# A decoder block's expert-table stage: instructions written out in turn, and four smaller edits

## The chip, the cores and the metric

The kernel runs on one core of a Trainium2 chip. The metric is device time in microseconds of one launch. One launch of the kernel before was also profiled; its trace is what the prediction reads. Five engines work side by side, each through its own instructions in order: TensorE (PE; PEld is its weight load), VectorE (DVE), ScalarE (ACT), GpSimd (POOL) and SyncE (SP, which here only issues DMAs). They wait for one another through semaphores.

## The reference

One decoder block on 1024 tokens of 1024 channels. Two mixers run side by side (an RWKV-7 recurrence and an attention over selected keys), are merged and normalised; then comes the part that matters here, a mixture of 16384 one-neuron experts:

```python
q = (ht @ w_pq).reshape(T, 8, 2, 64)                  # 8 heads, two half queries
s = jnp.einsum('thcd,hcnd->thcn', q, sub_keys)        # 128 first and 128 second keys
s1, i1 = lax.top_k(s[:, :, 0], 16); s2, i2 = lax.top_k(s[:, :, 1], 16)
cand = (s1[..., :, None] + s2[..., None, :]).reshape(T, 8, 256)
top_s, pos = lax.top_k(cand, 16)                      # 16 of 256 pairs
experts = take_along_axis(i1*128 + i2, pos)           # expert = first key * 128 + second key
gates = softmax(top_s)
act = gelu(einsum('cd,chkd->chk', h, u_tab[experts])) * gates
out = einsum('chk,chkd->cd', act, v_tab[experts])
```

A second residual and layer norm follow. Everything is float32.

## The kernel before

A scheduler puts the instructions of each engine in order when the program is built: it takes the order in which the code is written as priority and moves an instruction ahead where its own clock says that the earlier ones would still wait. On the chip each engine then keeps that order. Tiles come from pools with a fixed number of buffers (`bufs`); a new tile waits until the oldest buffer of that name is free.

The experts are computed in two ways. The first 384 tokens (three tiles of 128, `NG = 3`) are **gathered**: for each of 128 slots a row of 128 expert vectors is fetched with an indirect DMA on GpSimd (L1371, 512 KB each) into a room `g` and used by one VectorE instruction (L1375 for the dot with the token, L1379 for the weighted sum). These are 768 rows. Rows 0 to 127 are tied to earlier work, and row 300 (`MIDDLE`) is the first that may use a room of the last stage. Three rooms `g` serve them until then. The other 640 tokens (five tiles, 3 to 7) are **dense**: every expert is computed for every token and multiplied by a gate that is zero for experts not chosen. TensorE multiplies in float32 pieces: each operand is split into a high and a low part, ScalarE copying the high part (`whi`, L233) and GpSimd subtracting for the low part (`wlo`, L1272), and three products are added (L1285, L1287, L1289). One unit of dots, for 128 experts that share a first key, is 48 matmuls.

The stages around the change, in order of time:

- **Merge of the second half** (`merge`, H = 1). Eight output-projection units (L1044 on VectorE writes `vt`), a layer norm with transposes (L1063, L1108, L1114, L1070), then eight units of the expert queries (`wq`). Between units `next(side)` advances the retrieval of tiles 1 and 2, one of twelve steps after each of the first twelve units.
- **Retrieval** (`retrieve`): top 16 of each key half with MAX8, MATCH_REPLACE8 and FIND_INDEX8 on VectorE (L1136 to L1173), then the rank arithmetic: for each of six sums per tile `weighted` multiplies (L1190) and halves the 16 columns in four adds (L1192, L1194, L1195, L1196).
- **Table stage.** For each of the five dense tiles `gate_table` runs 16 steps of 8 tokens. A step makes two sets of one-hot rows: second keys in one instruction for eight tokens (L1247), first keys times gate for each token, six by VectorE (L1252) and two by two ScalarE instructions each (L1254, L1255). Eight float32 matmuls (L1259, two records each in the trace) give tables, which ScalarE copies from PSUM, transposing in its write (`st<-tp`, L233), and a DMA stores (`gtD`). The retrieval of tiles 3 to 7 feeds it; transposes (L1236) hand the found keys over. The same stage computes 69 units of dots ahead of their use (`dots_u`, stored by `dotD<-ds`) and gather rows 128 to 299. In the code the dots come after all tables and the gather at the very end of the program; the scheduler fills them in.
- **Dense stage.** For each of 16 groups of eight first keys: `dense_u` (dots, or `al`, the stored ones, then gelu, times the gate table `gt`, L1315, then split into `A`, the low part by L1317) and `dense_v` of the group before (eight units of 48 matmuls). Gate tables are loaded for four first keys at a time into two buffers (L1644, 1.3 MB each). In each group but the first the code puts one unit that is not stored ahead (`lead`) in front.

## Time and profile before

| | us |
|---|---|
| median of 3 runs | 3887.53 (3887.27 to 4839.4) |
| the profiled execution | 3874.22 |
| its span, first to last instruction | 3872.5 |
| PE / DVE / ACT / POOL busy | 3549.4 / 2759.5 / 1611.5 / 1992.2 |

Busy time is the union of an engine's instructions. Shares are averages over stages that differ much: the profile's slices show PE at nine tenths almost everywhere, and DVE at nine tenths or more only in the table stage. Times in the rows below count from the start of the span.

### The profile page before, as it was taken

The page shows a single profiled execution, that of the slowest core. Times are in us where ns is not written, and L with a number is a line of the kernel's source. Part 1 is how long each engine was busy: PE and PEld are TensorE (multiplying, and loading weights), DVE is VectorE, ACT ScalarE, POOL GpSimd, SP SyncE. Part 2 cuts the span into 40 slices and gives each one's busy share as a digit, 9 for nine tenths or more (in the row PEclk, how much of TensorE's full clock was granted, in tenths as well). Part 3 has the DMA queues.
Part 4 walks back from the last instruction along what each step waited for, and adds up shares of the span by engine and source line. Part 5 has one row for each costly group of instructions (what it writes and reads, how often), then busy time and mean ns, then how long its engine had stood idle before and what let it go on. Part 6 is the DMA issues. An engine that isn't in the chain of part 4 may idle for free.

```text
span 3872.5 us, 65040 instructions
## 1 busy us (share of the span) xinstructions
PE 3549.4 (92%) x24044; PEld 3172.0 (82%) x24045; DVE 2759.5 (71%) x5983; ACT 1611.5 (42%) x2909; POOL 1992.2 (51%) x1566
## 2 busy tenths in 40 slices
PE   8989999888999998779999898899999999999997
PEld 7667776665777776669889898899999999999997
DVE  7856644857377767779999999566676666676654
ACT  3558852343444443426455463622222232222222
POOL 5442222355455543254545454266676676776655
PEclk9999998999999999889999999999999999999998
DMA  7453334765676765477777777688898988998973
GB/s 231 148 151 103 103 98 143 280 188 183 192 222 219 218 220 170 140 258 261 243 259 252 258 273 248 234 301 314 310 332 317 330 313 323 335 323 318 322 266 115
DMA packets 434994, 920.97 MB, mean 238 GB/s; under 512 B 36356, under 2 KB 195412, under 8 KB 431732
## 3 DMA queue, kind: packets, MB, share of 16 engines
q1 hardware_dynamic: 311956, 498.38, 38.5%
q0 software_dynamic: 122720, 418.43, 31.0%
q8 instruction: 190, 3.11, 0.3%
q14 instruction: 128, 1.05, 0.1%
HBM read 791.59 MB, written 125.08 MB: 237 GB/s over the span
## 4 chain that ended last, share of the span: by engine, by line
PE 33%; DVE 21%; DMA 19%; issue 10%; POOL 9%; ACT 4%; SPq 1%; POOLq 0%; ACTq 0%; DVEq 0%
DMA g<-in_v_dram,gidx 4%; PE acc L425 4%; PE acc L426 4%; PE acc L427 4%; DMA g<-in_u_dram,gidx 4%; POOL g L1371 4%; POOL wlo L1272 4%; DVE pg L1379 3%; DMA raw<-in_vt_dram 3%; DMA gt<-gtD 3%; DVE gt L1252 3%; PE pair L1285 2%; PE pair L1287 2%; PE pair L1289 2%; DMA raw<-in_ut_dram 2%
## 5 line engine op out<-in xcount | busy, mean ns | idle before, releaser
L1272 POOL TENSOR_TENSOR wlo<-raw,whi 128x1024 fp32r<-128x1024 f32 x264 | 641.0, 2429 | 285.8 <-ACT whi L233 273.6
L415 POOL TENSOR_TENSOR wlo<-wraw,whi 128x512 fp32r<-128x512 f32 x280 | 372.5, 1333 | 564.0 <-ACT whi L233 496.7
L1371 POOL DMA_INDIRECT g<-in_u_dram,gidx x384 | 403.8, 1052 | 374.0 <-DVE g L1375 211.5
L1371 POOL DMA_INDIRECT g<-in_v_dram,gidx x384 | 388.0, 1011 | 378.3 <-DVE pg L1379 192.2
L1379 DVE SCALAR_TENSOR_TENSOR pg<-g,dots,pg 128x1024 f32<-128x1024 f32 x381 | 489.3, 1284 | 120.3 <-DMA g<-in_v_dram,gidx 113.9
L1285 PE MATMUL pair<-A,whi 128*128 128x320 f32 (+2 forms) x2048 | 483.0, 312 | 38.7 <-DVE A L1317 25.9
L1285 PE MATMUL pair<-h2T,whi 128*128 128x320 f32 x2048 | 479.1, 314 | 17.3 <-DMA h2T<-h2TD 10.0
L1287 PE MATMUL pair<-h2T,whi 128*128 128x320 f32 x2048 | 482.1, 315 | 3.7 <-DMA h2T<-h2TD 3.7
L233 ACT ACTIVATE whi<-raw 128x1024 fp32r<-128x1024 f32 x264 | 278.4, 1056 | 496.2 <-PE pair L1287 194.6
L1287 PE MATMUL pair<-A,whi 128*128 128x320 f32 (+2 forms) x2048 | 480.8, 311 | 0.0
L1289 PE MATMUL pair<-A,wlo 128*128 128x320 f32 (+2 forms) x2048 | 480.2, 311 | 0.5 <-POOL wlo L1272 0.5
L1289 PE MATMUL pair<-h2T,wlo 128*128 128x320 f32 x2048 | 480.4, 314 | 0.0
L1375 DVE SCALAR_TENSOR_TENSOR g<-g,pg 128x1024 f32<-128x1024 f32 x256 | 308.3, 1216 | 106.8 <-DMA g<-in_u_dram,gidx 104.6
L1285 PEld LDWEIGHTS pair<-A,whi 128*128 128x128 f32 x2048 | 348.8, 190 | 43.3 <-issue 29.6
L425 PE MATMUL acc<-big,whi 128*128 128x512 f32 x864 | 356.3, 413 | 23.5 <-DVE zs L533 7.1
L1285 PEld LDWEIGHTS pair<-h2T,whi 128*128 128x128 f32 x2048 | 348.3, 191 | 20.2 <-issue 11.0
L1287 PEld LDWEIGHTS pair<-h2T,whi 128*128 128x128 f32 x2048 | 349.5, 191 | 5.5 <-DMA h2T<-h2TD 4.0
L427 PE MATMUL acc<-big,wlo 128*128 128x512 f32 x864 | 350.7, 406 | 2.4 <-POOL wlo L415 2.4
L426 PE MATMUL acc<-big,whi 128*128 128x512 f32 x864 | 348.9, 404 | 3.6 <-DVE big L451 3.6
L1289 PEld LDWEIGHTS pair<-h2T,wlo 128*128 128x128 f32 x2048 | 348.8, 191 | 1.5
L1289 PEld LDWEIGHTS pair<-A,wlo 128*128 128x128 f32 x2048 | 348.8, 190 | 1.0 <-POOL wlo L1272 1.0
L1287 PEld LDWEIGHTS pair<-A,whi 128*128 128x128 f32 x2048 | 349.2, 190 | 0.0
(482 smaller groups left out, 6650.4 us busy)
## 6 DMA issues: line engine op xcount, KB each, us to landing
raw<-in_vt_dram SPq DMA_DIRECT2D x136, 512.0 KB
raw<-in_ut_dram SPq DMA_DIRECT2D x128, 512.0 KB
gtD<-st SPq DMA_DIRECT2D x20, 2048.0 KB
gt<-gtD SPq DMA_DIRECT2D x32, 1280.0 KB
wraw<-in_wz_dram SPq DMA_DIRECT2D x152, 256.0 KB
dotD<-ds SPq DMA_DIRECT2D x69, 320.0 KB
al<-dotD SPq DMA_DIRECT2D x69, 320.0 KB
mw<-in_wada_dram SPq DMA_DIRECT2D x32, 512.0 KB
```

The source lines that it names most:

```text
L233: copy = lambda o, i, **k: A.activation(o, i, AF.Copy, **k)
L415: G.tensor_tensor(lo, raw, hi.bitcast(F32), op=OP.subtract)
L425: mm(pt, lhsT=wh[:, ks], rhs=ah[:, k, :], start=k == 0, stop=False)
L426: mm(pt, lhsT=wh[:, ks], rhs=al[:, k, :], start=False, stop=False)
L427: ins = mm(pt, lhsT=wl[:, ks], rhs=ah[:, k, :], start=False, stop=k == nk - 1)
L1272: G.tensor_tensor(lo, raw, hi.bitcast(F32), op=OP.subtract)
L1285: mm(pts[n], lhsT=wh, rhs=ah[:, h], start=k == 0, stop=False)
L1287: mm(pts[n], lhsT=wh, rhs=al[:, h], start=False, stop=False)
L1289: mm(pts[n], lhsT=wl, rhs=ah[:, h], start=False, stop=last)
L1371: G.indirect_dma_start(out=u, out_offset=None, in_=a["u" if n < 2 else "v"], in_offset=bass.IndirectOffsetOnAxis(ap=idx[:, k:k + 1], axis=0))
L1375: V.scalar_tensor_tensor(u, u, 1.0, h2, op0=OP.mult, op1=OP.mult, accum_out=dots[:, k:k + 1])
L1379: V.scalar_tensor_tensor(acc, u, dots[:, k:k + 1], acc, op0=OP.mult, op1=OP.add)
```

## The change

- The table stage is written out in turn: 30 times one retrieval step, three table steps of each tile at hand, two units of dots and four gather rows; then eight times two table steps, one unit and four or no rows; then what is left. The gather becomes a generator (`gather_all`) that starts in this stage. Rows 128 to 299 use six rooms: three `g` and three `gx`.
- In a table step the first-key one-hots of eight tokens come from one bfloat16 comparison on VectorE (`hot`, against `keys8`, iota repeated eight times), and eight ScalarE copies multiply each by its gate. The two-instruction form on ScalarE, `iotan` and `ng` are gone. The matmuls write their columns to PSUM four apart, and the copy out of PSUM reads them in line and writes runs of four.
- In `weighted` one TENSOR_REDUCE takes the place of the four adds.
- In the second merge the twelve retrieval steps stand after every other unit, four of them in the `wq` loop.
- `h2T`, the dense tokens, is loaded in eight pieces (both parts of one 128-channel slice each) in place of two.
- `lead` is gone: the first keys of a group stand in their order, stored ones first.

```diff
-            if H or d % QS == QS - 1:
+            if H == 0 or d % 2:
                 next(side, None)
...
-            next(side, None)
+            if H == 0 or d % 2:
+                next(side, None)
...
             nc.sync.dma_start(qTD[H][:, h, :], qt)
+            if H and h % 2 == 0:
+                next(side, None)
...
-            V.tensor_tensor(pr[:, :, 0:8], pr[:, :, 0:8], pr[:, :, 8:16], op=OP.add)
-            s4 = tp_.tile([128, 64, 8], F32, name="wx")
-            V.tensor_tensor(s4[:, :, 0:4], pr[:, :, 0:4], pr[:, :, 4:8], op=OP.add)
-            V.tensor_tensor(s4[:, :, 0:2], s4[:, :, 0:2], s4[:, :, 2:4], op=OP.add)
-            V.tensor_tensor(dst, s4[:, :, 0], s4[:, :, 1], op=OP.add)
+            V.tensor_reduce(dst, pr, axis=AX.X, op=OP.add)
...
-            oh = du.tile([128, 16, 128], F32, name="gt", bufs=2)
-            V.tensor_tensor(oh[:, 0:8], iota[:, None, :].to_broadcast([128, 8, 128]),
-                            slots[:, 1, b * 8:b * 8 + 8, None].to_broadcast([128, 8, 128]), op=OP.is_equal)
+            room = du.tile([128, 20, 128], F32, name="gt", bufs=2)
+            oh2, oh1 = room[:, 0:8], room[:, 8:16]
+            hot = room[:, 16:20].rearrange("p a b -> p (a b)").bitcast(BF).rearrange("p (a b) -> p a b", b=8)
+            V.tensor_tensor(hot, keys8, k1[:, None, b * 8:b * 8 + 8].to_broadcast([128, 128, 8]), op=OP.is_equal)
+            V.tensor_tensor(oh2, iota[:, None, :].to_broadcast([128, 8, 128]),
+                            slots[:, 0, b * 8:b * 8 + 8, None].to_broadcast([128, 8, 128]), op=OP.is_equal)
             for t in range(8):
-                c = slice(b * 8 + t, b * 8 + t + 1)
-                if t < ONE_HOT:
-                    V.tensor_scalar(oh[:, 8 + t], iotan, slots[:, 0, c], slots[:, 2, c], op0=OP.is_equal, op1=OP.mult)
-                else:
-                    A.activation(oh[:, 8 + t], iota, AF.Square, bias=slots[:, 0, c])
-                    A.activation(oh[:, 8 + t], oh[:, 8 + t], AF.Relu, scale=ng[:, c], bias=slots[:, 2, c])
+                copy(oh1[:, t], hot[:, :, t], scale=slots[:, 1, b * 8 + t:b * 8 + t + 1])
             for u in range(2):
-                tp = ptp()
+                tp = ptp().rearrange("p (a b) -> p a b", b=4)
                 for t in range(4):
-                    mm(tp[:, t * 128:(t + 1) * 128], lhsT=oh[:, 4 * u + t], rhs=oh[:, 8 + 4 * u + t], start=True, stop=True)
+                    mm(tp[:, :, t], lhsT=oh2[:, 4 * u + t], rhs=oh1[:, 4 * u + t], start=True, stop=True)
                 t0 = b % 4 * 8 + 4 * u
-                copy(s_[:, :, t0:t0 + 4].rearrange("p a b -> p b a"), tp.rearrange("p (b a) -> p b a", b=4))
+                copy(s_[:, :, t0:t0 + 4], tp)
...
+        def room(row):
+            if EARLY <= row < MIDDLE and row % (GB + GX) >= GB:
+                return at["sl"].tile([128, 1024], F32, name="gx", bufs=GX)
...
-        for n in range(2):
-            G.dma_start(h2T[:, n], h2TD[:, n])
+        for k in range(8):
+            G.dma_start(h2T[:, :, k], h2TD[:, :, k])
...
+            def beside(tables, dots, n):
+                for g in list(found.values()):
+                    for _ in range(tables):
+                        next(g, None)
+                for _ in range(dots):
+                    next(ahead_, None)
+                for _ in range(n):
+                    next(rows)
+            steps = 6 * (8 - M1)
+            n = (MIDDLE - EARLY) // (steps + 6)
+            for k in range(steps):
+                next(side)
+                beside(3, 2, n)
...
+            for k in range(8):
+                beside(2, 1, n if k < 6 else 0)
...
-                    lead = next(i1 for i1 in first if i1 not in ahead)
-                    first = [lead] + [i1 for i1 in first if i1 != lead]
```

On VectorE, the start of the tables of tile 3, before (`pg<-g,dots,pg` is a gather row, `gt<-iota` the second keys, `gt<-iotan` the first keys):

```order
L1247 TENSOR_TENSOR gt<-iota,slots 128x1024
L1252 TENSOR_SCALAR gt<-iotan,slots 128x128 x6
L1379 SCALAR_TENSOR_TENSOR pg<-g,dots,pg 128x1024
L1247 TENSOR_TENSOR gt<-iota,slots 128x1024
L1252 TENSOR_SCALAR gt<-iotan,slots 128x128 x6
L1379 SCALAR_TENSOR_TENSOR pg<-g,dots,pg 128x1024 x2
```

The same place now (`gt<-keys_15512` is the bfloat16 comparison, `gx` one of the three new rooms):

```order
L1250 TENSOR_TENSOR gt<-iota,slots 128x1024
L1249 TENSOR_TENSOR gt<-keys_15512,slots 128x1024 x2
L1250 TENSOR_TENSOR gt<-iota,slots 128x1024
L1393 SCALAR_TENSOR_TENSOR pg<-gx,dots,pg 128x1024 x3
L1393 SCALAR_TENSOR_TENSOR pg<-g,dots,pg 128x1024 x3
L1249 TENSOR_TENSOR gt<-keys_15512,slots 128x1024
L1250 TENSOR_TENSOR gt<-iota,slots 128x1024
L1393 SCALAR_TENSOR_TENSOR pg<-gx,dots,pg 128x1024 x2
```

Six instructions per step have become one, and more gather rows stand between steps. Between one tile's hand-over to TensorE and the next, the four table cycles of the stage held 14.9 to 15.7 units of dots each in TensorE's order; now they hold 17.5, 15.8, 15.0 and 12.6, and VectorE's order 57, 51, 42 and 21 gather rows, 171 in place of 150.

On VectorE, the second merge where its layer norm begins (`lnst` is the norm, `vt` the last output projections, all else the retrieval), before:

```order
L1184 TENSOR_TENSOR ge<-wx,ranks 128x1024
L1190 TENSOR_TENSOR wp<-ge,df 128x1024
L1044 SCALAR_TENSOR_TENSOR vt<-acc,modc,xt 128x512
L1108 BN_STATS lnst<-rw 128x6
L1192 TENSOR_TENSOR wp<-wp 128x64x8
L1108 BN_STATS lnst<-rw 128x6 x2
L1194 TENSOR_TENSOR wx<-wp 128x64x4
L1109 BN_AGGR lnst<-lnst 128x2 x2
L1195 TENSOR_TENSOR wx<-wx 128x64x2
L1190 TENSOR_TENSOR wp<-ge,ranks 128x1024
```

And now:

```order
L1193 TENSOR_REDUCE i_14527<-wp 128x64
L1216 SCALAR_TENSOR_TENSOR i_14526<-i_14526,i_14527 128x128
L1218 CAST idx<-i_14526 128x128
L1042 SCALAR_TENSOR_TENSOR vt<-acc,modc,xt 128x512 x2
L1109 BN_STATS lnst<-rw 128x6 x3
L1110 BN_AGGR lnst<-lnst 128x2 x2
L1112 RECIPROCAL lnst<-lnst 128x1 x2
L1113 SCALAR_TENSOR_TENSOR lnst<-lnst 128x1 x2
```

The rank arithmetic of tile 2 no longer stands among the norm's instructions; it now comes behind them.

On SyncE, one group of the dense stage (`gt<-gtD` loads a gate table, `raw` weights, `al` stored dots), before:

```order
L1268 DMA raw<-in_ut_dram 128x1024 x2
L1308 DMA al<-dotD 128x640
L1644 DMA gt<-gtD 128x20x128
L1308 DMA al<-dotD 128x640
L1268 DMA raw<-in_vt_dram 128x1024 x3
L1644 DMA gt<-gtD 128x20x128
L1268 DMA raw<-in_vt_dram 128x1024 x2
```

And now:

```order
L1267 DMA raw<-in_ut_dram 128x1024
L1307 DMA al<-dotD 128x640
L1687 DMA gt<-gtD 128x20x128
L1267 DMA raw<-in_ut_dram 128x1024 x2
L1307 DMA al<-dotD 128x640
L1267 DMA raw<-in_vt_dram 128x1024 x3
L1307 DMA al<-dotD 128x640
L1267 DMA raw<-in_vt_dram 128x1024
L1687 DMA gt<-gtD 128x20x128
```

One load of the pair has moved ahead of the last dots of the group before, the other further behind, so that the two stand farther apart.

## Rows read from the trace of the kernel before

**Rows 1.** The page, part 1: busy us, share, instructions of each engine.

```profile
PE 3549.4 (92%) x24044; PEld 3172.0 (82%) x24045; DVE 2759.5 (71%) x5983; ACT 1611.5 (42%) x2909; POOL 1992.2 (51%) x1566
```

**Rows 2.** Windows: length, busy PE PEld DVE ACT POOL, granted clock, DMA share, GB/s.

```profile
1585.00:1615.00 30.00, 13.21 (x60) 10.54 (x61) 25.34 (x66) 20.71 (x35) 1.88 (x2) 0.61 0.15 50
1615.00:1665.00 50.00, 48.19 (x192) 37.84 (x192) 10.30 (x19) 17.19 (x30) 18.94 (x15) 0.93 0.65 210
...
1690.00:1753.00 63.00, 55.32 (x356) 54.79 (x355) 61.46 (x119) 16.81 (x20) 40.35 (x28) 0.91 0.81 264
1753.00:2411.00 658.00, 596.76 (x4088) 580.00 (x4088) 645.71 (x1634) 343.40 (x570) 323.79 (x210) 0.96 0.75 257
2411.00:2470.00 59.00, 39.55 (x275) 36.35 (x275) 49.52 (x119) 51.73 (x100) 3.25 (x1) 0.91 0.34 140
2480.00:2500.00 20.00, 20.00 (x138) 20.00 (x137) 5.46 (x7) 6.84 (x10) 5.41 (x5) 1.00 0.97 335
2470.00:3720.00 1250.00, 1213.61 (x8186) 1208.13 (x8187) 840.91 (x1038) 344.76 (x424) 838.52 (x626) 0.99 0.89 320
```

**Rows 3.** VectorE's groups in 1753 to 2411: busy us, mean ns, idle before.

```profile
L1252 DVE TENSOR_SCALAR gt<-iotan,slots 128x128 f32<-128x128 f32 x384 | 162.5, 499 | 0.0
L1379 DVE SCALAR_TENSOR_TENSOR pg<-g,dots,pg 128x1024 f32<-128x1024 f32 x108 | 138.3, 1281 | 5.8 <-DMA g<-in_v_dram,gidx 5.5
...
L1194 DVE TENSOR_TENSOR wx<-wp 128x256 f32<-128x256 bf16 x24 | 27.5, 1147 | 0.5
L1192 DVE TENSOR_TENSOR wp<-wp 128x512 bf16<-128x512 bf16 x24 | 21.4, 891 | 0.4
...
L1195 DVE TENSOR_TENSOR wx<-wx 128x128 f32<-128x128 f32 x24 | 13.9, 581 | 0.5
...
L1196 DVE TENSOR_TENSOR i<-wx 128x64 f32<-128x64 f32 x17 | 12.8, 755 | 0.2
L1184 DVE TENSOR_TENSOR ge<-wx,ranks 128x1024 bf16<-128x1024 bf16 x16 | 11.1, 693 | 0.5
```

**Rows 4.** Timelines of VectorE and GpSimd near 2120: start, us, engine, instruction, count.

```profile
2117.90 1.63 DVE L1252 TENSOR_SCALAR gt<-iotan,slots 128x128 f32<-128x128 f32 x6
...
2121.76 4.45 DVE L1252 TENSOR_SCALAR gt<-iotan,slots 128x128 f32<-128x128 f32 x6
2122.69 2.40 POOL L1272 TENSOR_TENSOR wlo<-raw,whi 128x1024 fp32r<-128x1024 f32 x1
```

**Rows 5.** Timeline of one table step of the last tile.

```profile
2453.74 1.93 ACT L233 ACTIVATE st<-tp 128x512 f32<-128x512 f32 x2
...
2454.81 2.07 PE L1259 MATMUL tp<-gt 128*128 128x128 f32 x16 [0.98 <-ACT st L233]
...
2455.47 0.65 ACT L1254 ACTIVATE gt<-iota,slots 128x128 f32<-128x128 f32 x2
2456.02 0.86 ACT L1255 ACTIVATE gt<-gt,slots,ng 128x128 f32<-128x128 f32 x2
2456.79 1.93 ACT L233 ACTIVATE st<-tp 128x512 f32<-128x512 f32 x2
```

**Rows 6.** TensorE's waits in 1753 to 2411: for whom, us, times, longest.

```profile
PE tp L1259 <- DVE gt L1252: 34.3, 19, 4.4
PE tp L1236 <- DVE i L1196: 24.8, 7, 7.4
```

**Rows 7.** ScalarE's timeline: copies out of PSUM, written in line.

```profile
1606.62 1.10 ACT L233 ACTIVATE big<-tp 128x512 f32<-128x512 f32 x2
```

**Rows 8.** The chain that ended last, 1584 to 1616, shares by line.

```profile
by line: DVE wp L1190 16.2%; DVE vt L1077 11.5%; ACT xn L1114 10.8%; DVE lnst L1108 7.8%; ACT wx L233 6.3%; PE tp L1070 6.1%; PE rw L1063 5.4%; DVE wp L1192 4.7%; DVE ge L1184 4.4%; DVE vt L1044 4.1%; DVE posb L1176 3.9%; DVE wx L1194 3.4%;
```

**Rows 9.** TensorE's timeline: the first matmul on the dense tokens.

```profile
1679.81 1.40 PE L1285 MATMUL pair<-h2T,whi 128*128 128x320 f32 x4 [10.02 <-DMA h2T<-h2TD]
```

**Rows 10.** Waits of TensorE and VectorE in the dense stage.

```profile
PE pair L1285 <- DVE A L1317: 29.5, 16, 6.6
DVE pair L1315 <- DMA gt<-gtD: 85.1, 16, 18.2
```

More of the change, by code (lines that the diff above doesn't have):

```diff
@@ L46 @@
 GM = 1
-QS = 1
+GX = 3
 TIES = 3
@@ L341, in rowb @@
         nc.sync.dma_start(dst, a["rows"][0:1, at:at + n].to_broadcast([parts, n]))
-    ident, iota, iotan = (base.tile([128, 128], F32, name=n) for n in ("ident", "iota", "iotan"))
+    ident, iota = (base.tile([128, 128], F32, name=n) for n in ("ident", "iota"))
     ranks = base.tile([128, 3, 16], BF, name="ranks")
@@ new lines, in by_slot, with gate_table @@
+        copy(dst[:, 0:2, :].rearrange("p a b -> p (a b)"), tp[:, 0:256])
+        copy(first_keys(dst), tp[:, 256:384])
+    first_keys = lambda slots: slots[:, 2, 0:64].bitcast(BF)
+    def gate_table(i, slots, sl, du, st, keys8):
+        k1 = first_keys(slots)
+        for b in range(16):
+            s_ = st[:, b // 4 % 2]
+            room = du.tile([128, 20, 128], F32, name="gt", bufs=2)
[4 more added lines that the diff above has]
+                            slots[:, 0, b * 8:b * 8 + 8, None].to_broadcast([128, 8, 128]), op=OP.is_equal)
+            for t in range(8):
+                copy(oh1[:, t], hot[:, :, t], scale=slots[:, 1, b * 8 + t:b * 8 + t + 1])
@@ L1342, in behind, with gather_all, peer_gather, index @@
         return nullcontext()
-    def peer_gather(i, du, dv, pg):
-        def index(at):
-            t = (gp if at < EARLY else du if at < MIDDLE else dv).tile([128, 128], U32, name="gidx")
+    def gather_all(at):
+        for i in range(NG):
+            acc = yield from peer_gather(i, at)
+            finish(i, acc, at)
+    def peer_gather(i, at):
+        pg = at["pg"]
+        def index(row):
+            t = (gp if row < EARLY else at["du"] if row < MIDDLE else at["dv"]).tile([128, 128], U32, name="gidx")
             nc.sync.dma_start(t, idxD[i])
             return t
+        def room(row):
+            if EARLY <= row < MIDDLE and row % (GB + GX) >= GB:
+                return at["sl"].tile([128, 1024], F32, name="gx", bufs=GX)
+            if row >= MIDDLE and row % (GB + GM) >= GB:
+                return at["dv"].tile([128, 1024], F32, name="g2", bufs=GM)
+            return grow()
         idx = None
@@ L1369, in peer_gather @@
                     idx = index(row)
-                u = grow() if row < MIDDLE or row % (GB + GM) < GB else dv.tile([128, 1024], F32, name="g2", bufs=GM)
+                u = room(row)
                 G.indirect_dma_start(out=u, out_offset=None, in_=a["u" if n < 2 else "v"],
@@ L1407, in out_rows, with finish @@
         nc.sync.dma_start(out[r0:r0 + n, :], dst[p])
-    def finish(i, acc, dv, rows):
+    def finish(i, acc, at):
         last = i == NG - 1
-        row, xa = ((dv.tile([128, 2 * DN], F32, name="A", bufs=AB)[:, 0:1024] if last else grow()) for _ in range(2))
+        row, xa = ((at["dv"].tile([128, 2 * DN], F32, name="A", bufs=AB)[:, 0:1024] if last else grow()) for _ in range(2))
         mod_row(row, 2)
@@ L1417, in finish @@
         V.tensor_tensor(y2, y2, xa, op=OP.add)
-        g, b = rows[0:2] if last else (grow(), grow())
+        g, b = at["ln"][0:2] if last else (grow(), grow())
         if not last:
@@ L1608, in body @@
             st = sl.tile([128, 2, 128, 32], F32, name="st")
+            keys8 = sl.tile([128, 128, 8], BF, name="keys8")
+            copy(keys8, iota[:, :, None].to_broadcast([128, 128, 8]))
             found = {}
@@ L1627, in body @@
                     pass
-            mark("dots")
-            for i1 in ahead:
-                ds = sl.tile([128, DN], F32, name="ds", bufs=4)
-                copy(by_half(ds), dots_u(i1, du, h2T, 2))
-                nc.sync.dma_start(dotD[ahead[i1]], ds)
+            for _ in ahead_:
+                pass
         tkp.__exit__(None, None, None)
@@ L1671, in body @@
             mark("gather")
-            for i in range(NG):
-                finish(i, peer_gather(i, du, dv, pg), dv, ln)
+            more.update(dv=dv, ln=ln)
+            for _ in rows:
+                pass
     mark("end")
```

35 lines of the change are left out of this document (19 added, 16 removed).

## The prediction

> **What bounds the kernel now.** I read the page's engine totals first: TensorE is busy 92% of the span [rows 1]. The change leaves TensorE's matmuls as they are, so what it can save is time in which TensorE stands idle or runs at less than its full clock. The windows by stage show where that is [rows 2]. In the dense stage, 2470 to 3720, TensorE works 1213.6 of 1250 us: 36 are left. In the four table cycles, 1753 to 2411, it works 596.8 of 658, while VectorE works 645.7, or 98%; so there VectorE sets the end. TensorE's waits say the same: 34.3 us for the first-key one-hots and 24.8 for the end of the rank sums, 59 of the 61 idle us [rows 6]. Ahead of them, 1585 to 1615 is the second merge's norm, where TensorE works 13 of 30 us at a granted clock of 0.61. In 2411 to 2470, the tables of the last tile, neither TensorE nor VectorE is full; ScalarE is, with 51.7 of 59.
>
> **Table cycles: VectorE.** VectorE's groups there give what goes and what comes [rows 3]. Six first-key one-hots per step go: 384 in 162.5 us. Their mean is 0.499, yet the timeline shows six in 1.63 us, 0.272 each, or six in 4.45 when GpSimd starts its 2.40 us subtraction among them [rows 4]. So 384 x 0.272 = 104 are work and 58 are stretch behind GpSimd. The stretch isn't bound to this instruction: L1194 takes 1.147 for 256 elements while the larger L1192 takes 0.891. The four adds go: 24 sums x (0.891 + 1.147 + 0.581 + 0.755) = 81 us.
>
> What comes is not in the trace. One bf16 comparison of 1024 elements per step: the nearest row is L1184, 1024 bf16 elements at 0.693; 64 x 0.69 = 44 (82 if it takes the 1.281 of the float32 row L1379). One reduce over 1024 elements per sum: I take the row L1379, the nearest of that length, 24 x 1.28 = 31 (17 at 0.69). By the new order the cycles hold 171 gather rows, now 150; 21 x 1.28, by L1379, is 27. Together 645.7 - 162.5 - 81 + 44 + 31 + 27 = 505. Some of the stretch moves to what now stands there, since GpSimd's subtractions stay; the removed bore 58 and, in the adds, perhaps as much (L1194 is longer than L1192 with half its elements). Of those 58 to 110 I take 60 back: VectorE then needs 565.
>
> Here a rule speaks against the edit of the rank sums. The Trainium skill, VectorE: DVE Perf Modes, Rules for kernel authors, says to expect tensor_reduce at the base rate, calls it the slowest operation of VectorE, and advises restructuring, which the four adds are. By the base rate the reduce costs about what L1379 does. Against the 3.37 us that the four adds take here, the rule loses 2.1 us a sum, so the trace favours the reduce.
>
> **Table cycles: TensorE.** A stored unit is 48 matmuls; 138 took 20.00 us in full flow [rows 2], so 6.96 us. A table step's 16 records take 2.07 [rows 5], a tile's sixteen 33. Adding some 6 us of retrieval matmuls to the new units per cycle gives 161, 149, 143 and 127 us. VectorE's 565, shared out by the rows of each cycle, are 158, 151, 140 and 115. The larger of each pair sum to 582. The two are now almost level, so they will wait for each other in turn: I keep 30 us of the 59, and 12 for a clock still below full (0.96 now). That makes 624 in place of 658, **34 gained** (0 to 66). The transfers are near their limit too: the first cycle moves 57 rows of 0.52 MB, 17.5 units of 0.83 and 8.4 of tables, 53 MB, or 166 us at the dense stage's 320 GB/s; that is within the 30. The six rooms I cost at nothing: waits for a row's landing were 5.8 us [rows 3]. The first stretch, 1690 to 1753, has VectorE at 61.5 of 63 too [rows 2]; it gains **3** (0 to 6).
>
> **Table step: ScalarE.** In the last tile a step lasts 3.05 us: two transposing copies, 1.93, and 1.12 for the four instructions on one-hots [rows 5]. No dots stand beside this tile in TensorE's order, before or now. Now ScalarE makes eight one-hots and two copies. One copy of 128 elements lies between 0.33 (half of L1254's 0.65) and 0.43 (half of L1255's 0.86): 0.38. A copy out of PSUM written in line takes 0.55 [rows 7] and the transposing one 0.96; writing runs of four should be near the first, 0.60. So 8 x 0.38 + 2 x 0.60 = 4.24, and 16 x 1.19 = **19 lost**. Bounds: 8 x 0.28 (1.12 over four) + 1.10 = 3.34, 5 lost; or 0.48 each for a read eight apart (a quarter of the 0.41 that a strided 512 costs, added) with 1.93 = 5.77, 44 lost.
>
> **The second merge.** The chain through 1584 to 1616 goes 32.6% through retrieval on VectorE (L1190, L1192, L1184, L1176, L1194) [rows 8], some 10 us, which stands among the norm's instructions. By the new order it comes behind them, in the wq loop, where VectorE works 10.3 of 50 us [rows 2] and TensorE covers it. I take **9** (0 to 12); if that cover is gone the steps return where tile 3's tables wait, and the gain is 0.
>
> **Loads of the dense tokens.** TensorE waits 10.02 us for `h2T` at its first matmul on them [rows 9]. With eight pieces the first matmul needs the first only, but GpSimd issues eight transfers and the last lands no earlier: **5** (0 to 10).
>
> **Dense stage.** Here 29.5 us of TensorE's waits are for the split product `A`, 16 times, and VectorE waits 85.1 us for a gate table's load, 16 times [rows 10]. In the old order the leading unit touches its table early, so the other table's load, which needs the room of the group's last use, lands late. In the new one the two loads stand further apart and the stored units come first. But the last unit of a group is now always a computed one, its product due soon after its dots. I take **8** gained (25 if most of 29.5 goes, 15 lost if each of the 16 waits grows by half).
>
> **Sum.** 34 + 3 - 19 + 9 + 5 + 8 = 40. The profiled execution took 3874.2, of which the span is 3872.5; 3834 is left. It ran 13.3 us below the median of the runs shown, 3887.5, which the forecast is compared with, so 3847. Removing `iotan` and `ng`, and making `keys8` once, cost nothing: they stand far ahead of the tables, where VectorE isn't full.
>
> **Rivals.**
>
> *Spread columns slow TensorE (slower).* The tables' matmuls now write four floats apart. No row of before has a matmul that writes so; rows give only 0.129 us a record for adjoining columns. If a record takes twice that, the 1024 records of the cycles cost 132 us more, and TensorE needs 194, 182, 176 and 160, together 712, with the 12 for the clock 724: 66 lost in place of 34 gained. The sum is 60 lost: 3934, by the median 3947. It decides from about 0.17 us a record, where 1024 x 0.04 us have eaten the whole 40. For it: the layout is new. Against it: a cycle's tables are 33 of TensorE's 127 to 161 us, the least of its work. The Trainium skill, PSUM — Partial Sum Buffer, Specifications, states this rule: PSUM has 8-byte cachelines, and any access pattern that isn't contiguous slows matmuls significantly. No row of before bears on it. 18%.
>
> *ScalarE becomes the bound.* If a step costs it 5.77, ScalarE's busy 343.4 in the cycles becomes 343 + 64 x 2.72 = 517, with the high-part copies queued behind the one-hots. It isn't full, but TensorE's weights are late, and the friction eats all but 4. With 44 lost in the tail: 4 + 3 - 44 + 22 = -15, 3889, by the median 3903. For it: ScalarE is already full in the last tile. Against it: in the cycles it has half its time free. 17%.
>
> *All of the relief arrives.* TensorE runs through the cycles in 592, with little friction, the tail loses 5, and the others give 3 + 12 + 10 + 25: 66 - 5 + 50 = 111; 3763, by the median 3776. For it: VectorE and TensorE each have less work than 592. Against it: their levels are close, and so are the transfers. 23%.
>
> **How the numbers follow.** The forecast has 42%; its own range is 3805 to 3885. The range 3765 to 3950 leaves out part of the third rival and about half of the first. A measurement of this kernel tells about 2% from no change, that is 3810 and 3965. Faster takes nearly all of the third rival and a little of the forecast, 0.27; slower takes a third of the first, 0.06; within 2% the rest, 0.67.
>
> **What would show it.** In the new trace: VectorE's busy share in the four cycles falls from 98% to about 90%, with TensorE's above 92%; the comparison at 0.7 to 1.3 and the reduce near 1.28 us; the table matmuls still at 0.13 a record; the last tile's step at 3.3 to 5.8, with ScalarE as what the tables wait for; the norm stretch 9 us shorter; the wait for `h2T` about 5. I am wrong in the main term if VectorE is still at 97%, or if the stretch by GpSimd has gone over whole to the new instructions; in the tail if a step is below 3.05; in the dense stage if the waits for `A` grow past 45 us.

## The result and the profile after

Median 3780.7 us of 4 runs (3771.6 to 3785.0) against 3889.5 before: ratio 0.9719, interval 0.9693 to 0.9745. Run again on another chip it took 3781.4 against 3876.8: 0.9751 (0.9729 to 0.9773). The forecast was 3847, 40 us gained; by the medians 109 were. One of the four runs before, at 4839.4, is left out of the ratio. The profiled execution took 3777.0, its span 3775.3, 97.2 below the span before. By the timelines of both, cut at TensorE's first matmul of each kind:

| stretch | before | after | gained | forecast |
|---|---|---|---|---|
| start to first dots | 1679.8 | 1660.3 | 19.5 | 14 |
| first dots to the last tile's first table | 738.8 | 661.3 | 77.5 | 37 |
| the last tile's tables | 50.5 | 68.5 | -18.0 | -19 |
| from there to the last dots | 1312.0 | 1296.5 | 15.5 | 8 |
| the rest | 91.4 | 88.6 | 2.8 | 0 |

Not all of the first row is the change's. VectorE's first output projection of the second merge, before and after:

```profile
1545.94 0.73 DVE L1044 SCALAR_TENSOR_TENSOR vt<-acc,modc,xt 128x512 f32<-128x512 f32 x1
...
1536.13 1.39 DVE L1042 SCALAR_TENSOR_TENSOR vt<-acc,modc,xt 128x512 f32<-128x512 f32 x2
```

From there to the first dots 133.9 us have become 124.2, 10 gained. The other 10 lie ahead of it, and there ten kernels that are alike so far (the changed one and nine of the experiments) spread from 1535.8 to 1544.2, so one trace of each can't tell them from chance.

The page's first part, after:

```profile
PE 3517.2 (93%) x24045; PEld 3146.2 (83%) x24045; DVE 2588.3 (69%) x5433; ACT 1695.7 (45%) x3230; POOL 1984.0 (53%) x1572
```

TensorE has as many matmuls as in [rows 1] but is busy 32 us less, and idle 65 us less. Where both come from is seen in the stretch between the first dots and the last tile's tables. Windows (length; busy PE, PEld, DVE, ACT, POOL; granted clock, DMA share, GB/s), first of before, then after:

```profile
1679.80:2418.60 738.80, 661.48 (x4488) 643.31 (x4488) 719.86 (x1814) 365.12 (x603) 365.13 (x239) 0.95 0.76 259
```

```profile
1660.30:2321.60 661.30, 637.38 (x4487) 619.97 (x4487) 576.37 (x1440) 428.28 (x854) 362.11 (x245) 0.99 0.80 293
...
2322.00:2391.00 69.00, 43.63 (x257) 40.27 (x257) 26.33 (x29) 67.71 (x158) 0.00 (x0) 0.81 0.22 94
...
2391.00:3686.00 1295.00, 1268.71 (x8589) 1265.85 (x8590) 873.71 (x1068) 360.27 (x441) 873.72 (x646) 0.99 0.89 319
```

The same 4488 matmuls take 661 us of busy time at a granted clock of 0.95 and 637 at 0.99: 24 of the 77 us. The other 53 are idle time: 77 before, 24 now. VectorE went from 97% to 87%, TensorE from 90% to 96%. TensorE's waits from 1737 to 2322 (for whom: us, times, longest), to be held beside [rows 6]:

```profile
PE tp L1258 <- ACT st L232: 8.8, 13, 1.8
PE tp L1233 <- DVE i L1193: 5.6, 4, 2.3
PE tp L1258 <- ACT gt L232: 3.4, 2, 2.9
```

The 59 us for VectorE have become 6. VectorE's groups in the same window (busy us, mean ns, idle before):

```profile
L1250 DVE TENSOR_TENSOR gt<-iota,slots 128x1024 f32<-128x1024 f32 x64 | 82.1, 1283 | 1.3 <-ACT slots L232 1.3
L1393 DVE SCALAR_TENSOR_TENSOR pg<-gx,dots,pg 128x1024 f32<-128x1024 f32 x52 | 66.6, 1281 | 0.6
L1393 DVE SCALAR_TENSOR_TENSOR pg<-g,dots,pg 128x1024 f32<-128x1024 f32 x52 | 66.5, 1279 | 1.9 <-DMA g<-in_v_dram,gidx 1.3
L1249 DVE TENSOR_TENSOR gt<-keys,slots 128x1024 bf16<-128x1024 bf16 x64 | 58.2, 914 | 16.7 <-issue 11.8 <-PE tp L1258 3.5 <-remote 1.3
...
L1191 DVE TENSOR_TENSOR wp<-ge,df 128x1024 bf16<-128x1024 bf16 x16 | 20.0, 1253 | 0.3
L1193 DVE TENSOR_REDUCE i<-wp 128x64 f32<-128x1024 bf16 x16 | 19.5, 1216 | 0.3
```

The reduce takes 1.22 (1.28 forecast), the comparison 0.914, and the multiply of the ranks has gone from 0.689 to 1.253: these two carry part of the stretch that the removed instructions bore. The last tile, on ScalarE's and TensorE's timelines (start, us):

```profile
2353.23 1.11 ACT L232 ACTIVATE st<-tp 128x512 f32<-128x512 f32 x2
...
2353.91 2.05 PE L1258 MATMUL tp<-gt 128*128 128x128 f32 x16 [2.23 <-ACT st L232]
2354.18 3.48 ACT L232 ACTIVATE gt<-gt,slots 128x128 f32<-128x128 bf16 x8
...
2357.50 1.13 ACT L232 ACTIVATE st<-tp 128x512 f32<-128x512 f32 x2
```

A step takes 4.27 us (2357.50 less 2353.23; 3.05 in [rows 5]). From start to start its two copies take 0.95 and its eight one-hots 3.32, or 0.42 each; the records, 1.11 and 3.48, overlap. The sixteen matmul records take 2.05, and 2.07 in [rows 5]: columns four apart cost nothing here. In the dense stage TensorE's waits for `A` and VectorE's for a gate table, beside [rows 10]:

```profile
PE pair L1284 <- DVE A L1316: 22.1, 7, 6.0
...
DVE pair L1314 <- DMA gt<-gtD: 19.4, 1, 19.4
```

One late table in place of sixteen.

### The profile page after: what moved, and what is told of

Same layout as the page of the kernel before. It is cut to its first block, busy times and chain, and to the rows that moved or that the text cites. A ratio compares the mean times of both kernels' runs of the same rounds, so it can differ in the third digit from the quotient of the medians.

```text
span 3775.3 us, 64780 instructions
## 1 busy us (share of the span) xinstructions
PE 3517.2 (93%) x24045; PEld 3146.2 (83%) x24045; DVE 2588.3 (69%) x5433; ACT 1695.7 (45%) x3230; POOL 1984.0 (53%) x1572
## 4 chain that ended last, share of the span: by engine, by line
PE 48%; DVE 16%; DMA 13%; ACT 9%; issue 7%; POOL 6%; SPq 0%; another core or an unknown queue 0%; POOLq 0%; ACTq 0%; DVEq 0%
PE pair L1286 7%; PE pair L1284 7%; PE pair L1288 7%; PE acc L423 4%; PE acc L424 4%; PE acc L425 4%; ACT gt L232 4%; DMA g<-in_u_dram,gidx 3%; DMA raw<-in_ut_dram 3%; DMA g<-in_v_dram,gidx 2%; POOL wlo L1271 2%; POOL g L1385 2%; DVE pg L1393 2%; PE acc L975 1%; DMA raw<-in_vt_dram 1%
## 5 line engine op out<-in xcount | busy, mean ns | idle before, releaser
L1385 POOL DMA_INDIRECT g<-in_u_dram,gidx x361 | 375.6, 1040 | 304.0 <-DVE g L1389 181.8
L1393 DVE SCALAR_TENSOR_TENSOR pg<-g,dots,pg 128x1024 f32<-128x1024 f32 x317 | 407.2, 1285 | 140.5 <-DMA g<-in_v_dram,gidx 131.9
L1284 PE MATMUL pair<-h2T,whi 128*128 128x320 f32 x2048 | 472.9, 311 | 5.8 <-DMA h2T<-h2TD 5.0
L1286 PE MATMUL pair<-h2T,whi 128*128 128x320 f32 x2048 | 473.1, 311 | 0.0
L1288 PE MATMUL pair<-h2T,wlo 128*128 128x320 f32 x2048 | 471.4, 311 | 1.7 <-POOL wlo L1271 1.7
L1385 POOL DMA_INDIRECT g<-in_v_dram,gidx x320 | 312.4, 976 | 167.7 <-DVE pg L1393 85.4
L1389 DVE SCALAR_TENSOR_TENSOR g<-g,pg 128x1024 f32<-128x1024 f32 x233 | 281.7, 1216 | 131.3 <-DMA g<-in_u_dram,gidx 125.5
L1284 PEld LDWEIGHTS pair<-h2T,whi 128*128 128x128 f32 x2048 | 343.1, 188 | 7.2 <-issue 5.1
L1286 PEld LDWEIGHTS pair<-h2T,whi 128*128 128x128 f32 x2048 | 343.3, 188 | 1.0
```

The costliest lines, as they stand in the source:

```text
L1284: mm(pts[n], lhsT=wh, rhs=ah[:, h], start=k == 0, stop=False)
L1286: mm(pts[n], lhsT=wh, rhs=al[:, h], start=False, stop=False)
L1288: mm(pts[n], lhsT=wl, rhs=ah[:, h], start=False, stop=last)
L1385: G.indirect_dma_start(out=u, out_offset=None, in_=a["u" if n < 2 else "v"], in_offset=bass.IndirectOffsetOnAxis(ap=idx[:, k:k + 1], axis=0))
L1389: V.scalar_tensor_tensor(u, u, 1.0, h2, op0=OP.mult, op1=OP.mult, accum_out=dots[:, k:k + 1])
L1393: V.scalar_tensor_tensor(acc, u, dots[:, k:k + 1], acc, op0=OP.mult, op1=OP.add)
```

## The experiments

The theory after the result (A): VectorE's work set the pace of the table stage, and what left VectorE is the gain. The rival (B): the written-out order and the rooms are the gain. "Stage" below is first dots to the end of the last tile's tables: 789.3 before, 729.9 after, 729.3 in the second run of the changed kernel. Ratios are to the kernel before, run on the same chip.

### Undoing the arithmetic, with the order kept

e1_adds puts the four adds back (and makes their result `start` bfloat16 again, as before):

```diff
-            V.tensor_reduce(dst, pr, axis=AX.X, op=OP.add)
+            V.tensor_tensor(pr[:, :, 0:8], pr[:, :, 0:8], pr[:, :, 8:16], op=OP.add)
...
+            V.tensor_tensor(dst, s4[:, :, 0], s4[:, :, 1], op=OP.add)
```

e2_onehot puts back the two forms of first-key one-hots (with `iotan`, `ng` and the negated keys that they need; the places in PSUM stay new), and e3_both does both:

```diff
-            V.tensor_tensor(hot, keys8, k1[:, None, b * 8:b * 8 + 8].to_broadcast([128, 128, 8]), op=OP.is_equal)
...
-                copy(oh1[:, t], hot[:, :, t], scale=slots[:, 1, b * 8 + t:b * 8 + t + 1])
+                if t < 6:
+                    V.tensor_scalar(oh1[:, t], iotan, slots[:, 2, c], slots[:, 1, c], op0=OP.is_equal, op1=OP.mult)
+                else:
+                    A.activation(oh1[:, t], iota, AF.Square, bias=slots[:, 2, c])
+                    A.activation(oh1[:, t], oh1[:, t], AF.Relu, scale=ng[:, c], bias=slots[:, 1, c])
```

Expected of e1_adds: 

> The changed kernel with the four adds per rank sum back in place of the reduce; nothing else is undone. Theory A (VectorE's work set the pace of the table cycles, and what the change took off it is the gain): VectorE gets 24 x 3.37 = 81 us back for the 29 of the reduces, 52 more on 504 of 585 us in the cycles, so it comes level with TensorE: 10 to 25 us slower than the changed kernel. Theory B (the written-out order and the six rooms are the gain, the fewer instructions ride along): within 5 us of the changed kernel.

Expected of e2_onehot: 

> The changed kernel with the old first-key one-hots (six TENSOR_SCALAR on VectorE, two by two ScalarE instructions); the reduce, the order, the rooms and the new places in PSUM stay. Theory A: in the cycles VectorE loses 58 us of bf16 comparisons and gets 104 (unstretched) to 162 (stretched): 46 to 104 more, so the cycles grow by 15 to 50 us; the last tile's step, 4.27 us now, falls to about 3.0, 20 us saved; together 5 faster to 30 slower. Theory B: only the last tile counts, 20 us faster than the changed kernel.

Expected of e3_both: 

> The changed kernel with both arithmetic edits on VectorE undone (four adds, old first-key one-hots): the written-out order, the rooms and the three small edits alone. Theory A: VectorE has about 630 to 690 us to do between the first and the last tile's tables and sets the pace again: 25 to 80 us slower than the changed kernel, the cycles back at VectorE 96 to 99% busy. Theory B: 20 us faster than the changed kernel (the last tile), the cycles still near 585 us.

Measured: e1_adds 0.9874 (0.9835 to 0.9913), stage 770.4; e2_onehot 0.9764 (0.9738 to 0.9789), stage 734.7; e3_both 0.9874 (0.9853 to 0.9894), stage 776.0. B fails: without the arithmetic the order, the rooms and the small edits give 13 us of the stage's 59. But A's sizes fail too. The adds cost 41 us of stage (and 6 more ahead of the first dots, see the small edits), not 10 to 25, though VectorE is busy no more than 84% in the cycles (523 of 620); TensorE's waits there, 1755 to 2375, tell most of it:

```profile
PE tp L1237 <- DVE i L1197: 35.3, 4, 21.4
PE tp L1262 <- ACT st L232: 5.5, 9, 1.7
```

Four waits, one at the end of each retrieval of tiles 4 to 7, the last of them 21.4 us long: a tile's tables can't begin before its last rank sum. They account for 30 of the 41 us (35.3 against 5.6). The one-hots, the largest single term of the prediction, are worth 5 us: 31 up to the last tile (692.4 against 661.3), less 26 that the old form saves in it (42.4 against 68.5).

### The arithmetic alone

The kernel before with the reduce, the comparison and its layout: no turn, three rooms, nothing of the small edits.

```diff
+            V.tensor_reduce(dst, pr, axis=AX.X, op=OP.add)
...
+            V.tensor_tensor(hot, keys8, k1[:, None, b * 8:b * 8 + 8].to_broadcast([128, 128, 8]), op=OP.is_equal)
...
+                copy(oh1[:, t], hot[:, :, t], scale=slots[:, 1, b * 8 + t:b * 8 + t + 1])
...
+                tp = ptp().rearrange("p (a b) -> p a b", b=4)
```

Expected: 

> The kernel before with the two arithmetic edits alone (reduce, bf16 comparison with gates by ScalarE and the new places in PSUM); the scheduler's own order, three rooms, the old merge, loads and lead. Theory A: the cycles lose most of VectorE's excess: 45 to 75 us faster than the kernel before. Theory B: 0 to 20 us faster or slower, since the last tile loses 18 and the order is the old one.

Measured: 0.9910 (0.9876 to 0.9945), some 35 us; stage 762.7. Neither theory has it: VectorE is busy 526 of 626 us in the cycles, and yet TensorE idles 56 between the first dots and the last tile. VectorE's waits in the cycles, 1735 to 2361:

```profile
DVE pg L1375 <- DMA g<-in_v_dram,gidx: 42.6, 29, 6.2
DVE v L1136 <- ACT sc L233: 19.2, 7, 4.5
DVE g L1371 <- DMA g<-in_u_dram,gidx: 17.6, 10, 5.5
```

60 us for rows to land. Before, in the cycles from 1760 to 2418, it was 11:

```profile
DVE pg L1379 <- DMA g<-in_v_dram,gidx: 5.5, 4, 2.0
DVE g L1375 <- DMA g<-in_u_dram,gidx: 5.1, 4, 2.2
```

A VectorE with less to do uses three rows up and waits for the next. A new theory, C: the rooms for rows are what lets the relief through.

### Rooms and turn, one at a time

e9_rooms takes the three `gx` from the changed kernel:

```diff
-            if EARLY <= row < MIDDLE and row % (GB + GX) >= GB:
-                return at["sl"].tile([128, 1024], F32, name="gx", bufs=GX)
```

e10_turn writes retrieval with the tables, then all dots, then the rows; e15_rooms_noturn does both:

```diff
-                beside(3, 2, n)
+                beside(3, 0, 0)
...
-            for k in range(8):
-                beside(2, 1, n if k < 6 else 0)
-            for _ in range(MIDDLE - EARLY - n * (steps + 6)):
-                next(rows)
...
             for _ in ahead_:
                 pass
+            for _ in range(MIDDLE - EARLY):
+                next(rows)
```

Expected of e9_rooms: 

> The changed kernel with three rooms for gather rows in place of six, the order still written out. Theory C (with VectorE relieved, the landing of rows takes over as what VectorE waits for: 60 us in the arithmetic-alone kernel against 3 in the changed one): VectorE's waits for rows in the cycles rise to 30 to 70 us and the kernel is 5 to 25 us slower than the changed one. My prediction, which costed the rooms at nothing: within 5 us.

Expected of e10_turn: 

> The changed kernel with the turn undone: retrieval and table steps written first, then the stored dots, then gather rows 128 to 299, filled in by the scheduler; the arithmetic, six rooms, merge, loads and dense order stay. Theory A (VectorE's work alone): within 10 us of the changed kernel. Interaction (relief of VectorE becomes time only where dots and rows stand in turn): TensorE idles 50 to 60 us from the first matmul on the dense tokens to the last tile's tables in place of 24, with a clock under full, and the kernel is 25 to 50 us slower than the changed one.

Expected of e15_rooms_noturn: 

> Turn undone and three rooms in place of six: both arithmetic edits and the small edits alone. If the rooms' worth doesn't hang on the turn: as with the turn, 50 to 65 us more from the first dots to the end of the last tile's tables than the 717 of the turn-undone kernel. If the scheduler, which may place dots where the rows would still be waited for, hides most of it: 20 to 40 us more, VectorE waiting 50 to 70 us for rows all the same.

Beside them the changed kernel ran again. Expected: 

> The changed kernel once more, on the chip of the three kernels beside it, so that small differences can be read: 2.5 to 3% faster than the kernel before, first matmul on the dense tokens at 1655 to 1670, then 661 us to the last tile's first table.

Measured: the changed kernel 3781.4 (first dots at 1660.9, 660.0 to the last tile's first table); e9_rooms 3840.9, 59 us slower (0.9917, 0.9886 to 0.9948), stage 792.5, no shorter than before's. The window from the first dots to the last tile in it, and the waits there of VectorE, ScalarE and TensorE:

```profile
1664.60:2388.50 723.90, 661.73 (x4487) 641.22 (x4488) 587.05 (x1434) 430.91 (x858) 354.56 (x243) 0.96 0.77 267
```

```profile
DVE pg L1391 <- DMA g<-in_v_dram,gidx: 62.8, 36, 5.9
DVE v L1137 <- ACT sc L232: 28.6, 8, 6.3
DVE g L1387 <- DMA g<-in_u_dram,gidx: 22.9, 9, 7.8
...
ACT gt L232 <- DVE gt L1249: 115.7, 38, 7.7
...
PE tp L1258 <- ACT st L232: 24.5, 14, 5.0
PE tp L1128 <- ACT st L232: 14.3, 7, 7.3
```

The same waits for rows and for the comparison in the changed kernel, with six rooms:

```profile
DVE g L1389 <- DMA g<-in_u_dram,gidx: 1.5, 1, 1.5
...
DVE pg L1393 <- DMA g<-in_v_dram,gidx: 1.3, 1, 1.3
...
ACT gt L232 <- DVE gt L1249: 58.0, 18, 5.9
```

85.7 us for rows in place of 2.8, with VectorE busy only 587 of 724. What is late on VectorE is handed on: ScalarE waits for the comparison, TensorE for ScalarE's copies out of PSUM (8.8 and 1.4 us with six rooms). TensorE idles 62 us and its busy time is back at 662, at a clock of 0.96. C holds, and by more than its 5 to 25 us. e10_turn: 0.9719 (0.9697 to 0.9742), 3768.1 us, 13 faster than the changed kernel beside it (3781.4; each of its five runs is shorter than any of that kernel's five); stage 717.2:

```profile
1668.30:2315.80 647.50, 627.66 (x4425) 612.02 (x4426) 579.67 (x1440) 427.76 (x857) 364.74 (x243) 0.99 0.81 297
```

TensorE idles 20 us there (24 with the turn), and 1.3 of the stored units, 9 us at 6.96, stand in the last tile, where it idles anyway. So the interaction that I expected of the turn isn't there; the turn costs 12, and those 9 are the larger part of it. e15_rooms_noturn: 0.9859 (0.9820 to 0.9898), stage 769.6; VectorE waits 71.5 us for rows. The rooms are worth 63 us with the turn and 52 without, so they need no turn; without it some 10 us of the waiting are hidden.

### Which arithmetic, once the turn is gone

The edits are those above: e13_adds_noturn is e10_turn with e1_adds, e14_onehot_noturn e10_turn with e2_onehot, e11_rooms_only e10_turn with both.

Expected of e13_adds_noturn: 

> Turn undone with the four adds in place of the reduce. With the turn they cost 41 us from the first dots to the end of the last tile's tables. If VectorE's work is what they cost (52 us on 580 of 648, spare time 68): 5 to 20 us slower than the turn-undone kernel. If it is the length of the chain at a tile's end, which no order hides: 25 to 45 us slower, with TensorE waiting 25 us or more for the rank sums.

Expected of e14_onehot_noturn: 

> Turn undone with the old first-key one-hots. With the turn they cost 31 us up to the last tile and gave 26 back in it. VectorE's work theory: 46 to 104 us more on 580 of 648, so 10 to 40 us slower up to the last tile, 26 faster in it: 15 faster to 15 slower than the turn-undone kernel. If the scheduler's order hides them: 20 to 26 us faster.

Expected of e11_rooms_only: 

> Turn undone, and both arithmetic edits undone too: six rooms and the small edits (merge, loads, lead) alone. If rooms are worth time only once VectorE is relieved (before, it waited 11 us for rows from the first dots to the last tile's tables): from the first dots to the end of the last tile's tables 745 to 785 us (789 before, 717 with the arithmetic), VectorE 96% busy or more, 25 to 45 us faster than the kernel before, all of it from the small edits. If rooms alone give the gain: near 717 and as fast as the kernel with the turn undone.

Measured: e13_adds_noturn 0.9842 (0.9811 to 0.9873), stage 765.1, 48 more than without the adds; TensorE waits 29.0 us for the rank sums in 5 waits, the longest 18.2, in place of 6.3. By that the chain is the larger part, with VectorE busy 600 of 696. 9 us more are the 1.3 units that no longer stand in the last tile; some 16 have no cause shown. e14_onehot_noturn 0.9740 (0.9710 to 0.9769), stage 735.9: 47 more up to the last tile (the same 9 among them), 28 less in it. e11_rooms_only 0.9868 (0.9839 to 0.9898), stage 769.7 with VectorE at 97% up to the last tile: rooms and small edits without the arithmetic take 20 off the stage, a third of what the rooms are worth with it. The whole gains 51 us, more than the 25 to 45 expected; its dense stretch, 1283.8, is the shortest of all.

All twelve side by side (stage, us; the kernel before and e5_arith have the old merge, loads and lead as well):

| arithmetic | turn, 6 rooms | 6 rooms | turn, 3 rooms | 3 rooms |
|---|---|---|---|---|
| reduce and comparison | 729.9 | 717.2 | 792.5 | 769.6; e5_arith 762.7 |
| reduce | 734.7 | 735.9 | | |
| comparison | 770.4 | 765.1 | | |
| neither | 776.0 | 769.7 | | before 789.3 |

### The small edits

In this order e4_lead; e6_merge (at its two places, with the steps of the `wq` loop taken out); e7_h2T, which e7b_h2T runs again:

```diff
+                else:
+                    lead = next(i1 for i1 in first if i1 not in ahead)
+                    first = [lead] + [i1 for i1 in first if i1 != lead]
...
-            if H == 0 or d % 2:
-                next(side, None)
+            next(side, None)
...
-        for k in range(8):
-            G.dma_start(h2T[:, :, k], h2TD[:, :, k])
+        for n in range(2):
+            G.dma_start(h2T[:, n], h2TD[:, n])
```

Expected of e4_lead: 

> The changed kernel with the leading unit of each dense group back. If the removal gave the dense stage's gain: VectorE's waits for gate tables come back (19 to about 85 us, 1 to 16 times) and the dense stage grows from 1295 by 8 to 16 us. If the dense stage gained for another reason (fewer gather rows left, another phase of the loads): within 4 us of the changed kernel.

Expected of e6_merge: 

> The changed kernel with the retrieval steps of the second merge after each of the first twelve units, as before. If their place gave the gain around the norm: the first matmul on the dense tokens comes 8 to 14 us later than at 1660 and the whole is as much longer. If VectorE's shorter rank sums gave it: within 4 us.

Expected of e7_h2T: 

> The changed kernel with the dense tokens loaded in two pieces. If the eight pieces gave the 5 us: TensorE waits about 10 and 4 us for them again, 5 to 8 us longer in all. If the first matmul was late for another reason: within 3 us.

Expected of e7b_h2T: 

> The changed kernel with the dense tokens loaded in two pieces, a second time, beside the changed kernel. If the wait at the first matmul is all (10 in place of 5 us): 4 to 8 us slower. If the late first dots throw the first table cycle out of step too, as the first look had it (92 us in place of 77 from the first dots to the first tables): 12 to 22 us slower.

e4_lead: 0.9777 (0.9743 to 0.9811); the dense stretch is 1310.2 in place of 1296.5, and VectorE's waits for tables are those of before:

```profile
DVE pair L1314 <- DMA gt<-gtD: 90.7, 16, 20.5
```

So the lead's removal gives some 14 us there; all three kernels with the lead (this one, e5_arith and before) take 1310 to 1312 in the dense stretch, the sixteen others 1284 to 1305.

The time from the first output projection to the first dots, free of what differs ahead of it, tells the edits of the merge and the loads apart:

| kernels | us |
|---|---|
| before | 133.9 |
| with everything that the change has there (ten) | 123.8 to 126.5 |
| the four adds back (e1, e3, e11, e13) | 130.0 to 132.4 |
| before with the arithmetic alone (e5_arith) | 131.1 |
| retrieval steps back (e6_merge) | 127.2 |
| loads in two pieces (e7_h2T, e7b_h2T) | 127.8, 129.7 |

So the reduce gives 3 (put alone into the kernel before) to 6 (taken out of the changed one) of the 10 us there, the loads 3 to 5, and the new place of the retrieval steps 1 to 3, which isn't clear of the spread. e6_merge as a whole: 0.9784 (0.9754 to 0.9814), the stretch from the first dots to the last tile 9 longer. e7_h2T: 0.9784 (0.9754 to 0.9814), TensorE's wait 9.9 us at the first dots for 5.0; again, e7b_h2T, 3797.2 us beside the changed kernel's 3781.4 (0.9797, 0.9774 to 0.9819), 16 us more, of which the wait at the first matmul is some 5. The first dots to the first tables take 92 and 86 us in the two, 76 and 77 with eight pieces, for one unit more; but e6_merge, with eight pieces, takes 86 for one unit more too, so what costs the other 11 us isn't shown. The profiled execution of e7b_h2T, the fastest of its six, was as short as the changed kernel's (3777.4 against 3776.7).

### The last tile

```diff
-                copy(oh1[:, t], hot[:, :, t], scale=slots[:, 1, b * 8 + t:b * 8 + t + 1])
+                gate = slots[:, 1, b * 8 + t:b * 8 + t + 1]
+                if i == 7 and t % 2:
+                    V.tensor_scalar(oh1[:, t], hot[:, :, t], gate, None, op0=OP.mult)
+                else:
+                    copy(oh1[:, t], hot[:, :, t], scale=gate)
```

e12_best is e8_tail and e10_turn together.

Expected of e8_tail: 

> The changed kernel with half of the last tile's first-key rows (every second token) multiplied by their gates on VectorE, which is busy 26 of the last 69 us of tables, in place of ScalarE. If ScalarE sets the last tile's pace (8 x 0.43 + 2 x 0.56 = 4.27 us a step): a step falls to about 3.0, and the kernel is 15 to 22 us faster than the changed one. If the PSUM rooms or TensorE's half clock set it: under 5 us.

Expected of e12_best: 

> Turn undone and the last tile's rows shared between VectorE and ScalarE. If both effects (13 us, and 24 us in the last tile) add: 3740 to 3750 us, 3.2 to 3.7% faster than the kernel before. If the dots that the last tile hid in the turn-undone kernel (1.3 units) come out again: 5 to 9 us of that are missing.

e8_tail: 0.9657 (0.9629 to 0.9685), 3747.5 us. The last tile takes 44.1 us, 24 fewer, which is above the 15 to 22 expected; its step is 2.71 (2355.45 less 2352.74):

```profile
2352.74 1.16 ACT L232 ACTIVATE st<-tp 128x512 f32<-128x512 f32 x2
...
2353.78 1.76 ACT L232 ACTIVATE gt<-gt,slots 128x128 f32<-128x128 bf16 x4
2354.58 1.10 DVE L1255 TENSOR_SCALAR gt<-gt,slots 128x128 f32<-128x128 bf16 x4
...
2355.45 1.15 ACT L232 ACTIVATE st<-tp 128x512 f32<-128x512 f32 x2
```

ScalarE did set the pace. (The expectation's 8 x 0.43 + 2 x 0.56 is 4.56; a step is 4.27 because the records overlap.) e12_best: 0.9674 (0.9638 to 0.9710), 3754.9 where 3740 to 3750 was expected; its stage is the shortest of all, 698.2 against e8_tail's 704.6. The 6 that it lacks of both effects together (704.6 less 12.7 is 692) are its last tile, 50.1 us for 44.1, in which the 1.3 units no longer fit for nothing. Their ratios overlap: which of the two is the faster can't be told. Both beat the changed kernel.

## Why the prediction was wrong in its size

- **The step that failed: the friction of the table cycles, with the rooms put at nothing.** "I keep 30 us of the 59, and 12 for a clock still below full", because VectorE at 565 and TensorE at 582 would be almost level and wait for each other in turn; and "The six rooms I cost at nothing: waits for a row's landing were 5.8 us". Between the hand-overs of tile 3 and tile 7, in the changed kernel and in e9_rooms:

```profile
1723.60:2318.10 594.50, 575.29 (x4091) 559.80 (x4090) 513.30 (x1243) 409.06 (x828) 315.07 (x213) 1.00 0.78 287
...
1737.90:2382.80 644.90, 582.77 (x3961) 562.96 (x3960) 522.99 (x1246) 406.44 (x822) 308.08 (x213) 0.96 0.75 264
```

TensorE's work came as priced, 575 for 580. The 42 us kept were 19, all of it idle time, at a clock of 1.00: 63 gained in place of 34. With three rooms 62 are idle, at 0.96, though VectorE is as far below TensorE as with six (523 and 583, 513 and 575). So what decides between the two is the landing of rows, not how near the levels of the two engines are. The wait of 5.8 us was short because VectorE was slow; with VectorE relieved and three rooms it is 71 to 86, and the stage is 770 to 792 in place of 717 to 730. By the spans the forecast missed 57 us. That the rooms' 52 to 63 are near it is in part chance, since the 42 kept already held some waiting: 29 of the 57 lie in the cycles, 11 beside them up to the last tile's first table, 14 ahead of the first dots, in the last tile and in the dense stretch, 3 in the rest.

- **VectorE's 565** was 513. I let 60 us of stretch return. The comparison got 64 x (0.914 - 0.693) = 14 and the rank multiplies 16 x (1.253 - 0.689) + 8 x (1.585 - 0.684) = 16; others lost a little: too high by half. And the 171 gather rows are the count from the first dots on; between the two hand-overs VectorE did 153, 18 fewer, some 23 us. (The sum ahead of the stretch comes to 504, not 505.)
- **The reduce** was priced as work, 50 us of 646, within one sum with the one-hots. Up to the last tile it is worth as much as they are, 33 to 48 us, though it saved 50 us of work by my prices and they 118, because it also shortens the chain behind which a tile's tables wait (35.3 and 29.0 us of TensorE's waits with the adds, 5.6 and 6.3 without). **The one-hots**, 162.5 us on VectorE, the largest group, are worth 31 to 47 there, but the last tile gives 26 to 28 back, which leaves 5 to 19. The Trainium skill's advice against the reduce (VectorE: DVE Perf Modes, Rules for kernel authors) would have kept the adds; the trace shows the reduce at 1.22 against 3.37 us. Most of the 3.37 is stretch: where no subtraction of GpSimd overlaps them, the four adds of before take 1.42 together.
- **The turn**, in which I saw the levelling of TensorE and VectorE, costs 12 us with the change's arithmetic (between -1 and 6 with less of it, 23 with three rooms). That the scheduler's own order does better wasn't among my rivals.
- **The last tile** was right in its mechanism, ScalarE's pace, and near in its size by luck: 4.24 a step forecast, 4.27 measured, 19 lost and 18 measured, but a one-hot takes 0.42 for the 0.38 forecast and a copy 0.48 for 0.60, and the two errors cancel. **Merge and loads** together 14: of the 19.5 to the first dots 10 lie where these edits are, and there the reduce, which my sum has only in the cycles, gives 3 to 6, the loads 3 to 5 for my 5, and the steps' new place 1 to 3 for my 9. **Dense** 8, measured 15.5, of which the lead is 14: right in kind, too small by half.
- **Rivals.** Spread columns: excluded, 2.05 us for sixteen records against 2.07. The Trainium skill's rule on access patterns in PSUM that aren't contiguous (PSUM — Partial Sum Buffer, Specifications) isn't borne out by the trace for these matmul writes at a stride of four. ScalarE as the bound: only in the last tile, where the forecast had it; in the cycles it is busy 409 of 594. "All of the relief arrives", 3776 by the median, is what happened in the cycles (594 us for its 592); its 5 lost in the last tile were 18 and its 25 in the dense stage 15.5. I gave it 23%, and held the nearness of the two engines' levels against it.

## What to carry to other kernels

Before a bound engine is relieved, look at what it hides: transfers that land just in time for a slow engine are late for a fast one, and the buffers that keep them in flight are then worth as much as the instructions removed. Count an edit by the chain that it shortens as well as by the work that it takes away: up to the last tile a group of 81 us at the end of each tile's chain was worth as much as the largest group, of 162. And look at where the removed work goes: the last tile, where ScalarE now sets the pace, took most of the latter's worth back. And try an order written by hand against the scheduler's own: here the buffers and the arithmetic gave the gain, and the order took a little of it back.

## What the runs showed of the hardware

- TensorE's busy time for the same 4488 matmuls is 661 us where it idled 77 (before) or 62 us (e9_rooms) among them, at a granted clock of 0.95 and 0.96, and 637 where it idled 24 (0.99). It isn't the sum of the idle time alone: e1_adds idles 61 us in the same stretch, 35 of them in four waits, and is busy 641, at 0.96. What decides wasn't tried.
- Matmuls that write PSUM four floats apart take as long as adjoining ones (2.05 and 2.07 us for sixteen records), and two copies out, read in line and written in runs of four, 1.11 us in place of 1.93 transposed.
- Eight ScalarE copies of 128 bf16 elements read eight apart take 3.48 us, 0.43 each; the 128 float32 elements in line of before's one-hots took 0.33 and 0.43 ([rows 5]).
- In the changed kernel's table stage a bf16 comparison of 1024 elements takes 0.69 us on the mean where no GpSimd subtraction overlaps it (69 of 80) and 2.03 where one does (11); the rank multiplies 0.69 (18 of 30) and 2.12 (12). The reduce stays at 1.21 and 1.22, a gather row at 1.28.
